# Moving every SBUF tile behind the constants by about 1.6 KB, onto multiples of 4 KB and 64 bytes

## The chip, the cores and the metric

The kernel runs on one core of one Trainium2 chip. The metric is the device time of one execution in microseconds (us), the median of several runs. A core has a matmul engine (PE, TensorE), whose weight loads are listed apart as PEld, a vector engine (DVE), a scalar engine (ACT), GpSimd (POOL) and a queue engine (SP) that issues all transfers here. The engines work on SBUF, a memory of 128 partitions; a tile has the same byte addresses in each partition, and "address" below means the byte offset inside a partition.

## What is computed

Two layers of a decoder trunk over 256 tokens of width 1024, in float32. Each layer is a SwiGLU feed-forward block, a token mixer (sliding-window attention beside an RWKV-7 state recurrence, joined by gates), and a second SwiGLU block, each followed by a residual layer norm:

```python
for l in range(DEPTH):
    x = layer_norm(ALPHA * x + 0.5 * swiglu(x, ffn_w_gu[l, 0], ffn_w_down[l, 0]), ln_g[l, 0], ln_b[l, 0])
    mix, v_first = token_mix(x, w_in[l], b_in[l], ...)
    x = layer_norm(ALPHA * x + mix, ln_g[l, 1], ln_b[l, 1])
    x = layer_norm(ALPHA * x + 0.5 * swiglu(x, ffn_w_gu[l, 1], ffn_w_down[l, 1]), ln_g[l, 2], ln_b[l, 2])
```

with `swiglu(x) = (silu(gate) * up) @ w_down`, `gate, up = split(x @ w_gu)`, 2816 hidden columns.

## The kernel before

**Products in three parts.** Each large product is made of three single-pass matmuls in the format fp32r: weights and activations are split into a high and a low part, and `mm3` adds high x high, high x low and low x high into one PSUM tile. `chunk` brings weights in pieces of 128 x 1024 floats: one transfer (or two) into a buffer `raw`, a cast on ACT into the high part, a subtraction on DVE into the low part. The parts go into the tiles `wh` and `wl` of the pool `wp`, three buffers each; in the feed-forward blocks (and the output projection) `deep=True` makes the chunks go round seven places, of which three are `wh`/`wl`, three lie in tiles of the pool `tp` that only the mixer uses otherwise, and one in the pair `rwh`, `rwl` of the pool `pp`. In the profile the tiles of the last four are all named `ws`. In the mixer all chunks are `wh`/`wl`.

```python
SPARE = (None, ("tp", "wG"), None, ("tp", "wuv", "wbkt"), None, ("tp", "war", "wbk"), ("pp", "rwh", "rwl"))

    def mm3(self, out, a, b, start, stop):
        mm = self.nc.tensor.matmul
        mm(out, a[0], b[0], start=start, stop=False)
        mm(out, a[0], b[1], start=False, stop=False)
        mm(out, a[1], b[0], start=False, stop=stop)
```

These three are lines 140, 141 and 142 of the profile. The second argument is the stationary operand (PEld reads 128 x 128 of it, 512 bytes of each partition), the third the moving one, which PE streams column by column, 4 bytes of each partition for a column.

**Two shapes.** Where the result is wanted with channels on the partitions (the body of the first feed-forward product, PSUM tile `accm`; the mixer's projections, `accm`; its two branch products, `accb`), the weights are stationary and the moving operand is 256 columns, 1024 bytes, of the activations: `xTh` and `xTl` for `accm`, `oTh`, `oTl`, `rwh`, `rwl` for `accb`. Where tokens are on the partitions (the first 512 hidden columns, the down projection, the output projection, PSUM tiles `acc` and `accg`), the activations (`mr`, `cum`, `gt0` and so on) are stationary and the moving operand is 512 columns, 2048 bytes, of a weight chunk. By the loops of the code there are 7104 of these fp32r matmuls: 4992 into `accm` (1536 of them in the mixers), 384 into `accb`, and 1728 with 512 columns. The small matmuls of attention and recurrence are plain fp32.

**Order.** Each engine works through its instructions in program order; in the mixer a table of numbers interleaves the recurrence with pieces of the projections. All transfers are issued from SP.

**Where tiles lie.** Four SBUF pools stand one behind another: `const` (identity, masks), `wp` (`raw`, `wh`, `wl`), `pp` (activations, parameters), `tp` (temporaries). A pool gives each tag as many buffers as it asks for, in the order of first use, and rounds each buffer up to 32 bytes. In front of `wp` stand the constants, among them `nhalf`, one float (4 bytes, 32 as rounded), so that what follows begins 32 bytes past a multiple of 64.

Of the kernel before, what the change touches and what calls it, by code (L numbers as in the profile page):

```python
# [9 lines left out]
F32 = mybir.dt.float32  # L10
# [5 lines left out]
P = 128  # L16
# [11 lines left out]
H = 8  # L28
# [3 lines left out]
NEG = -1e30  # L32
DECAY = math.exp(-0.5)
SPARE = (None, ("tp", "wG"), None, ("tp", "wuv", "wbkt"), None, ("tp", "war", "wbk"), ("pp", "rwh", "rwl"))
HT_TAGS = ("mr", "mk", "ma", "mep", "men", "mg", "cum", "mv", "gt0", "gt1", "gt2", "oTh")


# [12 lines left out]
VEC, VCOLS = {}, 0  # L50
# [6 lines left out]
class Trunk:  # L57
    def __init__(self, tc, ctx, ap):
        self.tc, self.nc, self.ap = tc, tc.nc, ap
        PS = bass.MemoryType.PSUM  # L60
        pool = lambda name, bufs, **kw: ctx.enter_context(tc.tile_pool(name=name, bufs=bufs, **kw))
        self.const = pool("const", 1)
        self.wp = pool("wp", 3)
        self.pp = pool("pp", 1)
        self.tp = pool("tp", 2)
        self.acc = pool("acc", 4, space=PS)
        self.sm = pool("sm", 3, space=PS)
        self.yp = pool("yp", 1, space=PS)
        self.dram = pool("dram", 1, space=bass.MemoryType.DRAM)
        self.n = self.nspare = 0  # L70
        self.first = []
        nc = self.nc
        self.ident = self.const.tile([P, P], F32, tag="ident", name="ident")
        nc.sync.dma_start(self.ident, ap["ident"])
        self.nhalf = self.const.tile([P, 1], F32, tag="nhalf", name="nhalf")
        nc.gpsimd.memset(self.nhalf, -0.5)

    def nm(self, s):
# [3 lines left out]
    def chunk(self, src, shape=(1, D), swap=False, deep=False, fine=1):  # L82
# [4 lines left out]
        if deep:  # L87
            spare = SPARE[self.nspare % len(SPARE)]
            self.nspare += 1
# [153 lines left out]
    def ffn(self, l, f, last, between=None):  # L243


        nc = self.nc
        hT = [[self.m4(HT_TAGS[6 * i + j], F32R) for j in range(6)] for i in range(2)]
        ps = [[None] * NT for g in range(2)]
# [63 lines left out]

    def load_vecs(self, l):

        vec = self.pp.tile([P, VCOLS], F32, tag="vec", name=self.nm("vec"))
        self.nc.sync.dma_start(vec, self.ap["vecs"][l])
        self.nc.gpsimd.tensor_scalar(vec[:, :NHALF], vec[:, :NHALF], 0.5, None, ALU.mult)
        return lambda name, i: vec[:, VEC[name] + i:VEC[name] + i + 1]

    def load_lora(self, l):  # L320
        nc, ap = self.nc, self.ap
        wa = self.pp.tile([P, 512], F32, tag="wa", name=self.nm("wa"))
        nc.sync.dma_start(wa[:64, :], ap["rw_w2"][l])
        nc.sync.dma_start(wa[64:, :], ap["rw_a2"][l])
        g2 = self.pp.tile([P, 512], F32, tag="g2", name=self.nm("g2"))
        nc.sync.dma_start(g2, ap["rw_g2"][l])
        v12 = None
        if l:
            v1 = self.pp.tile([P, 4, 32], F32, tag="v1", name=self.nm("v1"))
            nc.sync.dma_start(v1, ap["rw_v1"][l - 1].rearrange("(k p) r -> p k r", p=P))  # L330
            v2 = self.pp.tile([32, 512], F32, tag="v2", name=self.nm("v2"))
            nc.sync.dma_start(v2, ap["rw_v2"][l - 1])
            v12 = v1, v2
        sk = self.pp.tile([P, H], F32, tag="sink", name=self.nm("sink"))
        nc.sync.dma_start(sk, ap["attn_sinks"][l:l + 1, :].to_broadcast([P, H]))
        return wa, g2, v12, sk

# [694 lines left out]
```

## Time and profile before

| what | value |
|---|---|
| median of 3 runs | 1234.98 us (1234.7 to 1238.6) |
| the profiled execution's own time | 1237.51 us |
| its span, first to last instruction | 1235.6 us |
| PE busy, share of the span | 97% |
| PEld, DVE, ACT, POOL | 87%, 64%, 45%, 6% |
| mean granted TensorE clock | 0.996 of full speed |
| bytes moved, mean rate | 207.81 MB, 168 GB/s |

The span is what the profile divides into stages; the device time lies 1.91 us above it in that execution. "Busy" of an engine is the time in which at least one of its instructions was under way; since matmuls overlap each other, the distance from one matmul's start to the next tells more than the duration of one.

### The profile page before, as it was taken

The page shows a single profiled execution, that of the slowest core. Times are in us where ns is not written, and L with a number is a line of the kernel's source. Part 1 is how long each engine was busy: PE and PEld are TensorE (multiplying, and loading weights), DVE is VectorE, ACT ScalarE, POOL GpSimd, SP SyncE. Part 2 cuts the span into 40 slices and gives each one's busy share as a digit, 9 for nine tenths or more (in the row PEclk, how much of TensorE's full clock was granted, in tenths as well). Part 3 has the DMA queues.
Part 4 walks back from the last instruction along what each step waited for, and adds up shares of the span by engine and source line. Part 5 has one row for each costly group of instructions (what it writes and reads, how often), then busy time and mean ns, then how long its engine had stood idle before and what let it go on. Part 6 is the DMA issues. An engine that isn't in the chain of part 4 may idle for free.

```text
span 1235.6 us, 25429 instructions
## 1 busy us (share of the span) xinstructions
PE 1199.3 (97%) x10756; PEld 1075.5 (87%) x10756; DVE 792.4 (64%) x1174; ACT 550.9 (45%) x771; POOL 71.2 (6%) x96
## 2 busy tenths in 40 slices
PE   7999999999999999999999999999999999999997
PEld 5999888998789689998789998788987896999985
DVE  4555548967857866554666544588678588665544
ACT  5455434544434455443245444254354354554430
POOL 0000000211100000000000000012011000000000
PEclk9999999999999999999999999999999999999999
DMA  8777664442425577666377666364424255776661
GB/s 265 230 242 219 188 188 136 137 122 82 145 76 148 169 229 225 196 185 193 110 230 221 195 197 188 103 187 120 122 72 136 71 159 170 235 222 191 194 194 35
DMA packets 158001, 207.81 MB, mean 168 GB/s; under 512 B 8480, under 2 KB 133024, under 8 KB 157888
## 3 DMA queue, kind: packets, MB, share of 16 engines
q1 hardware_dynamic: 157888, 206.20, 55.1%
q8 instruction: 84, 1.38, 0.5%
q14 instruction: 29, 0.24, 0.1%
HBM read 205.12 MB, written 1.05 MB: 167 GB/s over the span
## 4 chain that ended last, share of the span: by engine, by line
PE 84%; DVE 7%; DMA 4%; issue 2%; ACT 2%; POOL 1%; SPq 0%; POOLq 0%; DVEq 0%; ACTq 0%
PE accm L140 15%; PE accm L142 15%; PE accm L141 15%; PE acc L140 9%; PE acc L141 9%; PE acc L142 8%; DMA raw<-in_w_out_dram 2%; DMA raw<-in_ffn_w_gu_dram 2%; DVE wl L119 1%; PE ps L133 1%; PE ps L724 1%; PE ps L715 1%; PE tr L151 1%; DVE ws L119 1%; PE y L133 1%
## 5 line engine op out<-in xcount | busy, mean ns | idle before, releaser
L119 DVE TENSOR_TENSOR wl<-raw,wh 128x1024 fp32r<-128x1024 f32 (+1 forms) x206 | 241.4, 1176 | 160.8 <-ACT wh L116 158.9
L116 ACT CAST wh<-raw 128x1024 fp32r<-128x1024 f32 x196 | 205.8, 1050 | 269.1 <-PE accm L141 121.0
L119 DVE TENSOR_TENSOR ws<-raw,ws 128x1024 fp32r<-128x1024 f32 (+1 forms) x178 | 201.9, 1139 | 172.2 <-ACT ws L116 170.6
L142 PE MATMUL accm<-xTh,wl 128*128 128x256 f32 x1000 | 286.2, 286 | 3.9 <-issue 2.3
L140 PE MATMUL accm<-xTh,wh 128*128 128x256 f32 x1000 | 289.9, 290 | 0.0
L141 PE MATMUL accm<-xTl,wh 128*128 128x256 f32 x1000 | 285.4, 285 | 0.0
L116 ACT CAST ws<-raw 128x1024 fp32r<-128x1024 f32 x164 | 171.8, 1049 | 204.8 <-DMA raw<-in_ffn_w_gu_dram 68.5
L140 PEld LDWEIGHTS accm<-xTh,wh 128*128 128x128 f32 x1000 | 191.4, 191 | 8.0 <-issue 6.0
L142 PEld LDWEIGHTS accm<-xTh,wl 128*128 128x128 f32 x1000 | 191.8, 192 | 5.1 <-DVE wl L119 2.0
L141 PEld LDWEIGHTS accm<-xTl,wh 128*128 128x128 f32 x1000 | 191.6, 192 | 2.0 <-issue 1.3
L140 PE MATMUL accm<-xTh,ws 128*128 128x256 f32 x664 | 184.0, 277 | 0.0
L142 PE MATMUL accm<-xTh,ws 128*128 128x256 f32 x664 | 183.7, 277 | 0.0
L141 PE MATMUL accm<-xTl,ws 128*128 128x256 f32 x664 | 183.6, 276 | 0.0
L140 PEld LDWEIGHTS accm<-xTh,ws 128*128 128x128 f32 x664 | 125.3, 189 | 0.1
L141 PEld LDWEIGHTS accm<-xTl,ws 128*128 128x128 f32 x664 | 124.6, 188 | 0.1
L142 PEld LDWEIGHTS accm<-xTh,ws 128*128 128x128 f32 x664 | 124.6, 188 | 0.0
L199 POOL TENSOR_SCALAR lnrs<-lnmv 128x1 f32<-128x1 f32 x12 | 5.6, 468 | 780.9 <-DVE lnmv L197 780.9
L142 PE MATMUL acc<-ws,gt 128*128 128x512 f32 x108 | 42.6, 394 | 0.0
L153 ACT CAST xTh<-tr 128x256 fp32r<-128x256 f32 x40 | 13.9, 372 | 55.5 <-PE tr L151 55.1
L142 PE MATMUL acc<-wh,gt 128*128 128x512 f32 x84 | 33.4, 398 | 0.0
L194 DVE SCALAR_TENSOR_TENSOR pre<-acc,x 128x512 f32<-128x512 f32 x24 | 16.5, 688 | 25.2 <-PE acc L142 25.1
L140 PE MATMUL acc<-wh,xTh 128*128 128x512 f32 x56 | 23.0, 413 | 8.0 <-ACT wh L116 7.6
(318 smaller groups left out, 2008.6 us busy)
## 6 DMA issues: line engine op xcount, KB each, us to landing
raw<-in_ffn_w_gu_dram SPq DMA_DIRECT2D x176, 512.0 KB, 4.6
raw<-in_ffn_w_down_dram SPq DMA_DIRECT2D x88, 512.0 KB, 4.3
raw<-in_w_in_dram SPq DMA_DIRECT2D x56, 512.0 KB, 4.4
raw<-in_w_in_dram SPq DMA_DIRECT2D x32, 256.0 KB, 3.1
raw<-in_w_out_dram SPq DMA_DIRECT2D x16, 512.0 KB, 4.4
raw<-in_w_branch_attn_dram SPq DMA_DIRECT2D x16, 256.0 KB, 4.0
raw<-in_w_branch_rwkv_dram SPq DMA_DIRECT2D x8, 512.0 KB, 4.1
lng<-in_ln_g_dram SPq DMA_DIRECT2D x6, 512.0 KB, 3.7
```

The lines of the kernel that those rows point to most:

```text
L116: nc.scalar.copy(wh, raw)
L119: nc.vector.tensor_sub(wl[:, c], raw[:, c], wh[:, c].bitcast(F32))
L133: ins = self.nc.tensor.matmul(*args, **kw)
L140: mm(out, a[0], b[0], start=start, stop=False)
L141: mm(out, a[0], b[1], start=False, stop=False)
L142: mm(out, a[1], b[0], start=False, stop=stop)
L151: nc.tensor.transpose(ps[:, i, :], x_sb[:, (k + i) * P:(k + i + 1) * P], self.ident)
L153: nc.scalar.copy(xh[o], ps[:, :m, :])
L194: nc.vector.scalar_tensor_tensor(pre[:, c], psums[h], scale / ALPHA, self.x[t][:, c], ALU.mult, ALU.add)
L199: nc.gpsimd.tensor_scalar(rs, mv[:, 1:2], LN_EPS / ALPHA ** 2, None, ALU.add)
L715: mm(ps[rb, m, :], ql[lv][rb, m, :], x[rb, m, :], start=True, stop=True)
L724: mm(ps[rb, m, :], bt[rb, m, :], z[rb, m, :], start=True, stop=True)
```

## The change

Three tiles are made larger, and only their first part is used: `nhalf` from 1 to 400 floats, `vec` from 82 to 96 floats, `sink` from 8 to 16 floats.

```diff
+NCONST = 400
-        self.nhalf = self.const.tile([P, 1], F32, tag="nhalf", name="nhalf")
+        self.nhalf = self.const.tile([P, NCONST], F32, tag="nhalf", name="nhalf")[:, :1]
-        vec = self.pp.tile([P, VCOLS], F32, tag="vec", name=self.nm("vec"))
+        vec = self.pp.tile([P, 96], F32, tag="vec", name=self.nm("vec"))[:, :VCOLS]
-        sk = self.pp.tile([P, H], F32, tag="sink", name=self.nm("sink"))
+        sk = self.pp.tile([P, 2 * H], F32, tag="sink", name=self.nm("sink"))[:, :H]
```

No instruction is added, removed or moved: on each of the five engines the built program has the same instructions with the same operands, sizes and waits in the same order. What differs is addresses. Everything behind `nhalf` moves up by 1568 bytes, what lies behind `vec` by 1600, and what lies behind `sink` by 1632. The places of the tiles that the fp32r matmuls read, as the allocator gives them:

| tiles | address before | past a multiple of 64 / of 512 | address after | past a multiple of 64 / of 512 |
|---|---|---|---|---|
| `raw`, `wh`, `wl`, three each | 23008 to 55776 in steps of 4096 | 32 / 480 | 24576 to 57344 | 0 / 0 |
| `xTh`, `xTl` | 59872, 68064 | 32 / 480 | 61440, 69632 | 0 / 0 |
| `oTl`, `mr`, `mk`, `ma`, `mep`, `men` | 80352, 92640 to 109024 | 32 / 480 | 81920, 94208 to 110592 | 0 / 0 |
| `mg`, `cum`, `mv`, `gt0`, `gt1`, `gt2`, `oTh` | 113184 to 137760 | 32 / 32 | 114752 to 139328 | 0 / 64 |
| `rwh`, `rwl` (also `ws`) | 141856, 145952 | 32 / 32 | 143424, 147520 | 0 / 64 |
| `wG`, `wuv`, `wbkt`, `war`, `wbk` (also `ws`) | 165280 to 189856 | 32 / 416 | 166912 to 191488 | 0 / 0 |

Some tiles began at multiples of 64 before already, among them `ident`, at 16512, and the mixer's `wa` and `g2`, at 150400 and 152448.

## Rows read from the trace of the kernel before

**Rows 1.** The page: engines, and the chain that ended last.

```profile
PE 1199.3 (97%) x10756; PEld 1075.5 (87%) x10756; DVE 792.4 (64%) x1174; ACT 550.9 (45%) x771; POOL 71.2 (6%) x96
...
PE 84%; DVE 7%; DMA 4%; issue 2%; ACT 2%; POOL 1%; SPq 0%; POOLq 0%; DVEq 0%; ACTq 0%
```

**Rows 2.** Stretches: us, busy (x instructions) by engine, granted clock, DMA share, GB/s.

```profile
110.00:180.00 70.00, 70.00 (x408) 61.36 (x408) 34.08 (x32) 30.08 (x31) 0.00 (x0) 1.00 0.66 195
240.00:405.00 165.00, 158.15 (x2485) 142.09 (x2484) 119.82 (x232) 70.85 (x129) 18.26 (x21) 0.99 0.42 122
500.00:580.00 80.00, 80.00 (x572) 74.79 (x571) 41.08 (x39) 36.06 (x39) 0.00 (x0) 1.00 0.63 192
```

**Rows 3.** PE, timeline, `wh`/`wl` stationary: start, us of one, instruction.

```profile
62.11 0.28 PE L141 MATMUL accm<-xTl,wh 128*128 128x256 f32 x1
62.23 0.28 PE L142 MATMUL accm<-xTh,wl 128*128 128x256 f32 x1
...
62.95 0.28 PE L142 MATMUL accm<-xTh,wl 128*128 128x256 f32 x1
```

**Rows 4.** The same, `ws` in the tiles of the pool `tp`.

```profile
63.19 0.28 PE L141 MATMUL accm<-xTl,ws 128*128 128x256 f32 x1
63.30 0.28 PE L142 MATMUL accm<-xTh,ws 128*128 128x256 f32 x1
...
64.21 0.28 PE L141 MATMUL accm<-xTl,ws 128*128 128x256 f32 x1
```

**Rows 5.** The same, `ws` in `rwh`, `rwl`, in two passes over them.

```profile
67.12 0.28 PE L142 MATMUL accm<-xTh,ws 128*128 128x256 f32 x1
...
68.48 0.28 PE L142 MATMUL accm<-xTh,ws 128*128 128x256 f32 x1
...
70.03 0.28 PE L140 MATMUL accm<-xTh,ws 128*128 128x256 f32 x1
...
71.33 0.28 PE L142 MATMUL accm<-xTh,ws 128*128 128x256 f32 x1
```

**Rows 6.** The same, 512 moving columns: from `wh`/`wl`, and from `tp`.

```profile
140.00 0.39 PE L141 MATMUL acc<-wl,mr 128*128 128x512 f32 x1
...
142.09 0.39 PE L141 MATMUL acc<-wl,mr 128*128 128x512 f32 x1
...
142.78 0.39 PE L141 MATMUL acc<-ws,mr 128*128 128x512 f32 x1
...
144.86 0.39 PE L141 MATMUL acc<-ws,mr 128*128 128x512 f32 x1
```

**Rows 7.** Plain fp32 on PE: timeline of two windows, and durations min/median/max in ns.

```profile
219.34 0.92 PE L133 MATMUL psl<-xg,g 128*128 128x256 f32 x3
219.34 1.99 PE L133 MATMUL psl<-xg,g 128*128 128x256 f32 x8
...
205.67 0.60 PE L537 MATMUL tr<-ident,gt 128*128 128x128 f32 x4
L537 PE MATMUL tr<-ident,gt x16: 271/273/329, 205.7 to 819.2; 128*128 128x128 f32 x16
```

**Rows 8.** Groups of the page, and `accm` in the two mixers (PE, PEld, DVE, ACT).

```profile
L142 PE MATMUL accm<-xTh,wl 128*128 128x256 f32 x1000 | 286.2, 286 | 3.9 <-issue 2.3
L140 PE MATMUL accm<-xTh,ws 128*128 128x256 f32 x664 | 184.0, 277 | 0.0
...
184.00:425.00 241.00, 106.74 (x768) 96.29 (x768) 1.91 (x4) 13.14 (x28) 0.99 0.42 124
794.00:1042.00 248.00, 107.91 (x768) 96.75 (x768) 1.91 (x4) 13.16 (x28) 0.99 0.41 122
```

**Rows 9.** The page: transfers by tile, number, KB each, us to landing.

```profile
raw<-in_w_in_dram SPq DMA_DIRECT2D x32, 256.0 KB, 3.1
g<-in_rw_g_dram SPq DMA_DIRECT2D x2, 256.0 KB, 3.2
```

## Prediction

> **What bounds the kernel now.** I read the page first: PE is busy for 97% of the span, and 84% of the chain that ended last is PE's [rows 1]. Then the stretches, since that average covers several stages. In the feed-forward blocks PE has no idle time at all (70.00 of 70.00 us, 80.00 of 80.00), while DVE and ACT are busy for half of it or less and transfers for about two thirds; in the mixer PE still works 158.15 of 165 us [rows 2]. So a nanosecond per matmul counts some thousand times, and a gain on any other engine counts only where a stage begins. The granted clock is 1.00 in the feed-forward blocks, the level of 2.4 GHz: a column then lasts 0.417 ns, 256 columns 106.7 ns, 512 columns 213.3 ns.
>
> The timeline of PE shows that it does not reach this. With `wh` and `wl` stationary, seven steps from 62.11 to 62.95 take 0.84 us: 120.0 ns for a matmul of 256 columns [rows 3]. With the `tp` tiles stationary, nine steps from 63.19 to 64.21 take 1.02 us: 113.3 ns [rows 4]. Shape, moving operand and engine are the same; what differs is where the weights lie. With `rwh` and `rwl` it is 113.3 ns in one pass (1.36 us for twelve steps) and 118.2 in another (1.30 us for eleven) [rows 5]. With 512 columns moving it is 232 ns from `wh`/`wl` and 231 from `tp` (2.09 and 2.08 us for nine steps) [rows 6]. Plain fp32, which takes two passes of the clock per column, behaves otherwise: 128 columns in (600 - 273) / 3 = 109 ns, 256 columns in (1.99 - 0.92) / 5 = 0.214 us [rows 7], hence 256 or 512 clock steps and about 2.5 ns. The moving operand there is `ident`, at a multiple of 64, or `xg`, 32 past one, and neither shows more than that.
>
> **How I read these numbers.** 113.3 and 120.0 are 106.7 plus once and twice 6.67 ns, and 6.67 ns is 16 columns, or 64 bytes of a partition. I take SBUF to hand PE 64 bytes of a partition at a time, with just enough speed for one fp32r column per clock. Then 1024 bytes that begin 32 past a multiple of 64 touch 17 such lines, and 17 x 6.67 is 113.3; plain fp32 asks for half that rate, so an extra line is hidden there. The second 6.67 ns comes where the weights that PEld reads for the next matmul meet the moving operand. In the table of addresses, `wh`, `wl`, `xTh` and `xTl` all lie 480 past a multiple of 512 (their inner steps are 512 and 1024 bytes): both streams begin on the same line of the 512, and one gives way once. `tp` lies 64 bytes lower (416), `rwh` 64 higher (32), and the collision is absent or now and then there. This is inference: before, every fp32r operand is 32 past a multiple of 64, so no row shows an aligned one.
>
> **The change part by part.** The larger tiles cost no work: the same instructions, and the unused parts are neither loaded nor set. Transfers and the other engines see new addresses too. 256 KB into `g2`, at a multiple of 64 before, land after 3.2 us and 256 KB into `raw`, 32 past one, after 3.1 [rows 9]; packets differ in length, but nothing there speaks for alignment, and a fraction of 3 us at each of about a dozen stage starts would be a few us at most, so I enter nothing. DVE and ACT are covered by PE, being busy for half the time [rows 2].
>
> For PE, two edits in opposite directions:
>
> *The line.* All fp32r operands begin at multiples of 64, so a matmul of 256 columns needs 16 lines, not 17, and one of 512 needs 32, not 33. That is 6.67 ns for each, down to a floor of 109 (or 214 to 216) ns by rows 7. Bounds from rows: nothing, if the 6.67 ns has another cause; the whole distance to the floor, if alignment ends the collisions too.
>
> *The collision.* `wh` against `xTh` stays at distance 0, `rwh` at 64. The `tp` tiles go from 64 below `xTh` to distance 0 (3072 and 0 past a multiple of 4096, both 0 past one of 512). By rows 3 and 4 that costs these matmuls 6.67 ns. Bounds: 0, and 6.67.
>
> Counts: 3 x 1000 matmuls with `wh`/`wl`, of which 2 x 768 in the mixers, and 3 x 664 with `ws` [rows 8], three quarters of them in `tp` (1494) and one quarter in `rwh`/`rwl` (498); by the code 384 into `accb` and 1728 with 512 columns. So:
>
> 1. `wh`/`wl`, feed-forward: 1464 x 6.67 = 9.8 us saved (120.0 to 113.3).
> 2. `wh`/`wl` and `accb` in the mixers: 1920 x 6.67 = 12.8 us. There the recurrence's chain passes DVE and ACT, and these matmuls fill its gaps; PE is idle for 4% [rows 2]. Some of the gain turns into longer waits; between 0 and 12.8 I take half, 6.4 us.
> 3. `ws` in `tp`: one line less, one collision more: 0.
> 4. `ws` in `rwh`/`rwl`: 113.3 to the floor of 109, 498 x 4.3 = 2.1 us.
> 5. 512 columns: 1728 x 6.67 = 11.5 us, between 0 and two lines, 23.0 (231 is nearer to 34 or 35 lines than to 33, so these collide anyway).
>
> Sum: 29.8 us. The profiled execution took 1237.51 us with a span of 1235.6; the median of the runs, 1234.98, is 2.5 below it, and I count from the median: **1205 us**. With terms 2 and 5 at their ends it is 1187 to 1223.
>
> **The rivals.**
>
> *Only the distance counts, and the 17th step is no matter of alignment* (a cost at each matmul's end that is rounded up to whole lines would look the same). Then the line term is 0, and the `tp` tiles, moved into step with `xTh`, go from 113.3 to 120.0 ns: 1494 x 6.67 = 10.0 us, all in feed-forward blocks where PE is never idle, so **1245 us**. It decides as soon as fewer than about 1500 of the other matmuls gain a line. For it: rows 3 and 4, which show the distance at work and nothing on alignment. Against it: 113.3 is 17 lines without remainder.
>
> *Addresses matter only in the large, or not at all.* `wh` and `xTh` lie within 40 KB of each other, `tp` 100 KB away; if near tiles collide, a move by 1.6 KB changes nothing: **1235 us**, within 0.3% (3.7 us, about what a measurement of this kernel can tell from no change). Against it: `rwh`, 80 KB from `xTh`, shows both 113.3 and 118.2 [rows 5]. [...]
>
> *Alignment ends collisions as well.* Then all go to the floor: 3000 x 11, 1494 x 4.3, 498 x 6 and 384 x 9 ns are 33, 6.4, 3.0 and 3.5 us, 1728 x 16 ns are 27.6: 73 us, less half of the mixers' 20: 63 us, **1172 us**. For it: plain fp32 reaches this floor. [...] Against it: two streams on one line must still take turns.
>
> **How the numbers follow.** The forecast gets 0.48, the floor 0.20, the distance alone 0.20, no effect 0.12. Faster by over 0.3%: 0.68; within it: 0.12; slower: 0.20. To leave out no more than 2 in 10 the range must reach both outer cases: 1172 to 1246, the likeliest case's own being 1187 to 1223.
>
> **What would show each step.** PE's timeline in a feed-forward body: 113.3 ns with `wh`, 113.3 with `tp`, 109 with `rwh`/`rwl`, about 225 with 512 columns, and plain fp32 as before. Right on the line but wrong on the collision: `tp` at 109. The first rival: 120 with both `wh` and `tp`, 231 with 512. The floor: 109 and 216 throughout. If PE idles longer in the feed-forward blocks, with more waits for `raw`, transfers could not follow the faster PE: 512 KB for twelve matmuls at 225 ns are 194 GB/s, against 195 GB/s in rows 2 with a third of the transfer time free, so I don't expect it. The prediction fails most easily if the 6.67 ns is no line.

## The result: 0.7% slower, and the profile after

The changed kernel took 1244.54 us (median of 4 runs, 1243.76 to 1246.68) against 1235.56 for the kernel before beside it (4 runs): a ratio of 1.0072, with an interval of 1.0047 to 1.0097. (Ratios here are those on record and differ slightly from the quotients of the medians; an interval is the 95% one.) The forecast was 1205 us; the rival in which only the distance between tiles counts gave 1245.

The page of the changed kernel (line numbers are two higher than before): the engines, and two groups of matmuls with 256 columns (busy us, mean ns of one, idle before); 512 of the 1000 in the first group belong to the mixers.

```profile
PE 1207.9 (97%) x10756; PEld 1086.5 (87%) x10756; DVE 792.8 (64%) x1174; ACT 552.1 (44%) x771; POOL 72.5 (6%) x96
...
L142 PE MATMUL accm<-xTh,wh 128*128 128x256 f32 x1000 | 290.2, 290 | 0.0
...
L142 PE MATMUL accm<-xTh,ws 128*128 128x256 f32 x664 | 188.0, 283 | 0.0
```

PE has grown by 8.6 us over [rows 1] and its weight loads, PEld, by 11.0; the other engines by 1.3 us at most. Of PE's groups on the page, the one with `ws` as weights has grown, to 283 ns for one from 277 [rows 8]. The one with `wh` has not; before it was:

```profile
L140 PE MATMUL accm<-xTh,wh 128*128 128x256 f32 x1000 | 289.9, 290 | 0.0
```

The timeline of PE after the change shows the steps.

```profile
61.88 0.28 PE L142 MATMUL accm<-xTh,wh 128*128 128x256 f32 x1
...
62.48 0.28 PE L144 MATMUL accm<-xTh,wl 128*128 128x256 f32 x1
62.60 0.28 PE L142 MATMUL accm<-xTh,ws 128*128 128x256 f32 x1
...
63.92 0.28 PE L144 MATMUL accm<-xTh,ws 128*128 128x256 f32 x1
...
70.13 0.28 PE L142 MATMUL accm<-xTh,ws 128*128 128x256 f32 x1
...
71.19 0.28 PE L142 MATMUL accm<-xTh,wh 128*128 128x256 f32 x1
```

With `wh` it is 0.60 us for five steps, 120 ns, as in [rows 3]: no line was saved. With a `tp` tile (62.60 to 63.92) it is 1.32 us for eleven steps, 120 ns, where [rows 4] had 113.3. With `rwh`/`rwl` (70.13 to 71.19) it is 117.8 ns for nine steps, the slower of the two states in [rows 5].

Over the whole trace the mean step went like this. Steps of more than 200 ns (300 with 512 columns) are left out, and a step counts for the weights of the matmul that begins at its end. The order of the chunks gives 1488 matmuls with `tp` tiles and 504 with `rwh`/`rwl`, where the prediction took three quarters and one quarter, 1494 and 498.

| weights, columns | number | before, ns | after, ns | change x number, us |
|---|---|---|---|---|
| `tp`, 256 | 1488 | 114.05 | 119.98 | +8.8 |
| `rwh`/`rwl`, 256 | 504 | 114.51 | 117.70 | +1.6 |
| `wh`/`wl` in feed-forward blocks, 256 | 1464 | 119.41 | 119.98 | +0.8 |
| `wh`/`wl` in the mixers, 256 | 1536 | 119.63 | 119.67 | +0.1 |
| all with 512 columns | 1728 | 231.61 | 230.49 | -1.9 |

The sum is +9.4 us; the spans differ by 9.3 (1244.9 and 1235.6), the medians by 9.0.

### The profile page after: what moved, and what is told of

It is laid out like the page before. It is cut to its first block, busy times and chain, and to the rows that moved or that the text cites. A ratio compares the mean times of both kernels' runs of the same rounds, so it can differ in the third digit from the quotient of the medians.

```text
span 1244.9 us, 25429 instructions
## 1 busy us (share of the span) xinstructions
PE 1207.9 (97%) x10756; PEld 1086.5 (87%) x10756; DVE 792.8 (64%) x1174; ACT 552.1 (44%) x771; POOL 72.5 (6%) x96
## 4 chain that ended last, share of the span: by engine, by line
PE 83%; DVE 8%; DMA 3%; issue 2%; ACT 2%; POOL 1%; SPq 0%; POOLq 0%; DVEq 0%; ACTq 0%
PE accm L142 16%; PE accm L144 15%; PE accm L143 15%; PE acc L144 8%; PE acc L143 8%; PE acc L142 8%; DMA raw<-in_w_out_dram 2%; DVE wl L121 1%; PE ps L135 1%; DMA raw<-in_ffn_w_gu_dram 1%; PE ps L726 1%; ACT wh L118 1%; PE tr L153 1%; PE ps L717 1%; DVE lnst L197 1%
## 5 line engine op out<-in xcount | busy, mean ns | idle before, releaser
L142 PE MATMUL accm<-xTh,ws 128*128 128x256 f32 x664 | 188.0, 283 | 0.0
L144 PE MATMUL accm<-xTh,ws 128*128 128x256 f32 x664 | 187.6, 282 | 0.0
L143 PE MATMUL accm<-xTl,ws 128*128 128x256 f32 x664 | 187.6, 282 | 0.0
L142 PEld LDWEIGHTS accm<-xTh,ws 128*128 128x128 f32 x664 | 127.4, 192 | 0.1
L144 PEld LDWEIGHTS accm<-xTh,ws 128*128 128x128 f32 x664 | 126.8, 191 | 0.0
```

## The experiments

Theory D: what a step costs hangs on the distance, within a period of some hundred bytes, between the tile that PEld reads and the one that PE streams. In the diffs, `gap` is a tile that nothing reads or writes; it is made before all others of its pool, and moves every later tile.

**Alignment alone, from the kernel before.**

```diff
+        self.wp.tile([P, 8], F32, tag="gap", name="gap_wp", bufs=1)
```

> All tiles from the pool wp on move up by 32 bytes, so that every fp32r operand begins at a multiple of 64 as in the changed kernel, but all distances between them stay as they were before (wh to xTh 0, tp to xTh 64 lower). Theory D (only the distance between the stationary and the moving tile counts): 120.0 ns per matmul of 256 columns with wh, 113.3 with the tp tiles, 1235 us as before (within 4). Rival A (begins at multiples of 64 are themselves what slows the changed kernel): tp at 120, about 1244 us. The forecast's line theory, if something in the changed kernel merely hid its gain: wh at 113.3, tp at 109, about 1200 us.

Measured: 1234.99 us against 1234.90, ratio 1.001 (0.9995 to 1.0025). Timeline of PE, 256 columns, all operands at multiples of 64:

```profile
61.75 0.28 PE L142 MATMUL accm<-xTl,wh 128*128 128x256 f32 x1
...
62.35 0.28 PE L141 MATMUL accm<-xTh,ws 128*128 128x256 f32 x1
...
62.58 0.28 PE L143 MATMUL accm<-xTh,ws 128*128 128x256 f32 x1
...
63.60 0.28 PE L143 MATMUL accm<-xTh,ws 128*128 128x256 f32 x1
```

Five steps of 120 ns with `wh` and nine of 113.3 with a `tp` tile, as before. The line term of the prediction is gone, and so is rival A.

**Distance alone, from the kernel before.**

```diff
+        self.tp.tile([P, 16], F32, tag="gap", name="gap_tp", bufs=1)
```

> Only the pool tp moves, by 64 bytes; all fp32r operands stay 32 past a multiple of 64, and tp comes to distance 0 from xTh. Theory D: tp at 120.0 ns, wh at 120.0, rwh/rwl at 113 to 118 as the phase at their start has it, about 1244 us (1494 x 6.67 = 10 us over before). Rival A: nothing is aligned, so tp stays at 113.3 and the time at 1235 us.

Measured: 1244.32 us, ratio 1.0083 (1.0064 to 1.0102). 64 bytes in front of one pool do what the whole change does:

```profile
63.09 0.28 PE L141 MATMUL accm<-xTh,ws 128*128 128x256 f32 x1
...
64.41 0.28 PE L143 MATMUL accm<-xTh,ws 128*128 128x256 f32 x1
```

Eleven steps of 120 ns with a `tp` tile that lies at distance 0 and is not aligned.

**The distance taken back, in the changed kernel.**

```diff
+        self.tp.tile([P, 112], F32, tag="gap", name="gap_tp", bufs=1)
```

> The changed kernel with the pool tp moved by another 448 bytes, so that its tiles lie 64 below xTh again as before the change; every fp32r operand keeps a multiple of 64. Theory D: tp back to 113.3 ns and wh at 120, 1235 us, the same as before within 0.3%. If anything but the distance of tp slowed the changed kernel, part of its 9 us stays.

Measured: 1234.58 us against 1234.74, ratio 0.9992 (0.9979 to 1.0005); `tp` at a mean of 114.06 ns, `wh`/`wl` at 119.6. Nothing of the 9 us stays.

**The other tiles moved apart, from the kernel before.**

```diff
+        self.pp.tile([P, 16], F32, tag="gap", name="gap_pp", bufs=1)
```

> All of the pools pp and tp move by 64 bytes against wp: wh and wl come to lie 64 below xTh and xTl, where the tp tiles lay and stay. Theory D: 113.3 ns with wh as with tp; 1464 matmuls in feed-forward blocks x 6.67 = 9.8 us saved, 1536 in the mixers x 6.67 = 10.2 us of which half counts, rwh/rwl now entered from a free phase and at 113.3 (about 1 us): about 1219 us (1214 to 1225). Rival R (matmuls collide with tiles that lie near, whatever the distance modulo 512): wh stays at 120 ns and the time at 1235 us.

Measured: 1226.73 us, ratio 0.9939 (0.992 to 0.9957): faster, but 8 us where 16 were expected. Rival R falls: in the feed-forward blocks `wh`/`wl` went from 119.4 to a mean of 114.0 ns. In the mixers they went only to 117.2. The timeline of a feed-forward block shows what lies behind it:

```profile
452.22 0.28 PE L141 MATMUL accm<-xTh,ws 128*128 128x256 f32 x1
...
453.28 0.28 PE L141 MATMUL accm<-xTh,ws 128*128 128x256 f32 x1
...
457.02 0.28 PE L142 MATMUL accm<-xTl,ws 128*128 128x256 f32 x1
...
457.61 0.28 PE L141 MATMUL accm<-xTh,ws 128*128 128x256 f32 x1
...
458.29 0.28 PE L141 MATMUL accm<-xTh,wh 128*128 128x256 f32 x1
...
459.65 0.28 PE L141 MATMUL accm<-xTh,ws 128*128 128x256 f32 x1
...
489.57 0.28 PE L141 MATMUL accm<-xTh,wh 128*128 128x256 f32 x1
...
490.93 0.28 PE L141 MATMUL accm<-xTh,ws 128*128 128x256 f32 x1
491.04 0.28 PE L142 MATMUL accm<-xTl,ws 128*128 128x256 f32 x1
...
492.29 0.28 PE L141 MATMUL accm<-xTh,wh 128*128 128x256 f32 x1
```

At one distance, 64 below, nine steps take 1.06 us (117.8 ns) soon after a stage has begun, and twelve take 1.36 (113.3) later, with `wh` as with `tp`. So there are two states. At 457.02 and 457.61 PE is in a pass over `rwh`/`rwl`, which lie 64 above `xTh`, and the state changes within it: five steps of 118 ns up to 457.61, then six of 113.3 up to 458.29, and 113.3 with `wh` and all that follows. By the trace's starts it is so in all four feed-forward blocks: each begins at 117.8 ns or returns to it after the small fp32 matmuls `tr`, changes for the last time in such a pass or at its start, and stays at 113.3 to its end. The mixers have no such chunk, their runs are short, and each begins after small fp32 matmuls; about one in five or fewer of their steps were below 115.5 ns, against four in five or more in the feed-forward blocks.

**Three sweeps of the distance.** `wh` and `wl` are made 32 or 64 bytes wider, so that their three buffers lie at three distances, and gaps set where these begin (the first sweep's edit without its gap in `tp`; the others differ in widths and gaps):

```diff
-            wh = self.wp.tile([P, 1024], F32R, tag="wh", name=self.nm("wh"), bufs=3)
-            wl = self.wp.tile([P, 1024], F32R, tag="wl", name=self.nm("wl"), bufs=3)
+            wh = self.wp.tile([P, 1032], F32R, tag="wh", name=self.nm("wh"), bufs=3)[:, :1024]
+            if not self.n_gap:
+                self.n_gap = self.wp.tile([P, 104], F32, tag="gap2", name="gap2", bufs=1)
+            wl = self.wp.tile([P, 1032], F32R, tag="wl", name=self.nm("wl"), bufs=3)[:, :1024]
```

> The three buffers of wh, and those of wl, lie 96, 64 and 32 bytes below xTh and xTl (modulo 512), and the tp tiles 32 below. If SBUF hands out 64 bytes at a time and collisions are between such pieces, 32 below touches the same piece at half of the time and costs 3 to 7 ns, 64 and 96 below cost nothing (113.3 ns). If the pieces are 32 bytes or less, 32 below costs nothing either and all show 113.3 ns. Time about 1219 us if nothing at 32, 1235 or more if 32 collides like 0.

> The three buffers of wh, and those of wl, begin 256 above, 192 below and 128 below xTh and xTl (modulo 512), the tp tiles 128 below. Theory D with a period of 512 bytes: only distance 0 collides, so 113.3 to 118 ns at all three, and about 1225 us. Theory D with a period of 128 (two lines of 64 taking turns): 128 and 256 are like 0, 120 ns; only 192 is free; about 1245 us.

> The same with 64, 128 and 192 above, and the tp tiles 64 above. Period 512: 113.3 to 118 ns everywhere, about 1225 us. Period 128: 64 and 192 at 113.3 to 118, 128 at 120 ns, and about 1232 us. If the sign counts (64 above showed 113.3 or 118 by its entry, 64 below mostly 113.3), tp at 118 and 1230 us or more.

Measured, one execution each and so without an interval: 1235.47 us (against a median of 1234.9), 1238.12 and 1227.06 (against one execution at 1234.7). Mean steps of 256 columns, worked out from the starts as above, feed-forward blocks and mixers together (bytes by which the weights lie above `xTh`/`xTl`; the column for 0 is from the runs before):

```
 distance   -256   -192   -128    -96    -64    -32      0    +64   +128   +192
 wh, wl    119.5  115.2  118.5  119.9  116.2  116.9  119.6  114.6  118.4  114.9
 tp                      118.5         114.1  116.9  120.0  113.7
```

Neither expected period is right. 0 and 256 are the same, 128 is nearly as dear, and odd multiples of 64 are cheap on either side; 32 is between, and 96, which was to cost nothing, is as dear as 0.

**The disputed steps by themselves.** 62 blocks of 24 matmuls ahead of the kernel's own work; the weights begin `d` above the moving operand, which begins `m` bytes into a tile that lies 32 past a multiple of 64, and has `n` columns. The inner loop:

```diff
+            for _ in range(24):
+                self.nc.tensor.matmul(ps[:, :n], st[:, a:a + P], mv[:, b:b + n], start=True, stop=True)
```

> Ahead of the kernel's own work stand 62 blocks of 24 fp32r matmuls on two weight tiles, whose results nobody reads; the kernel's own result is as before, its time longer by about 180 us. In a block all steps are alike: the weights begin d bytes above the moving operand (modulo 512), which begins m bytes into its tile and has n columns. Theory D: 120 ns at d = 0 and 113 to 118 at d = 64 and 448, with 256 columns; between 0 and 64 a slope or a jump tells how wide the piece is that collides. The 17th step: if it is a fixed cost at each matmul, (n + 16) / 2.4 ns for every n of 128 or more; if it is one step in 17, n / 2.4 x 17 / 16 ns, 56.7 at 128 and 226.7 at 512; if it is a line more because the operand begins 32 past a multiple of 64, it vanishes at m = 32 (109 ns), which the aligned kernel already speaks against.

Timeline of two blocks, `d` = 64 and `d` = 256 (`n` = 256; runs of equal matmuls are one row, with the time from the first start to the last end):

```profile
21.13 2.10 PE L171 MATMUL probe<-wh,wh 128*128 128x256 f32 x17
...
43.73 2.08 PE L171 MATMUL probe<-wh,wh 128*128 128x256 f32 x16
```

(2.10 - 0.28) / 16 is 114 ns, (2.08 - 0.28) / 15 is 120. Means of the last 16 steps of each block, from the trace's starts; the distances stood twice, in rising and in falling order:

```
 d, n=256     0     32     64     96    128    160    192    224    256    320    384    448
 rising           118.4  113.4  117.4  120.2  119.9  113.4  116.7  120.0  117.8  118.6  117.8
 falling  120.3   118.4  117.8  118.5  118.7  120.0  117.8  116.7  120.0  113.3  118.8  117.8

 n          192    240    272    320    384    448    512
 d=64            112.1  123.4  146.7  173.4  202.1  233.4
 d=448    111.7  111.6  126.7  146.7  173.3  200.1  228.7
```

(Two blocks are left empty: the first, whose early steps took 213 ns, and one at a granted clock of 0.56. Left out are those of 64 and 128 columns, and distances of 16, 48, 80, 112 and 480, at 118 to 120 ns.) Odd multiples of 64 take 113.3 or 117.8 ns at one and the same distance; 0 and 256 take 120. At `d` = 64, operands that begin at `m` = 32, a multiple of 64, or at 16 or 48 settle at 113.3 ns, as one 32 past it. Only `m` = 4, which begins both operands 36 bytes past a multiple of 64, takes 120.0, at `d` = 64 and at 448 (where the other three take 117.8 to 118.3). And 113.3 is no line more. A column takes 0.417 ns: (200.1 - 146.7) / 128 between 320 and 448 columns at `d` = 448, at a granted clock of 1.00. What a matmul takes over its columns is neither fixed nor one part in 16, but 6.7 ns at 256 columns, 13.4 at 320 and 384 and 15 to 20 at 512 for these two distances, while 192 and 240 columns, 80 and 100 ns by themselves, take 112. The expectation had none of this, and its 180 us more were 196.

**Fewer weights.** The same with 256 or 512 moving columns and fewer columns of weights, `w`. The inner line:

```diff
+                        self.nc.tensor.matmul(ps[:w, :n], st[:, d // 4:d // 4 + w], mv[:, :n], start=True, stop=True)
```

> Blocks of 24 matmuls ahead of the kernel's own work, their results unread, with 256 or 512 moving columns and 128, 96, 64 or 32 columns of weights, at distances of 64, 0 and 192 bytes. Theory W (the 17th step and the collisions belong to the weight load: it reads 512 bytes of a partition for each matmul, and in the blocks of 192 and 240 columns the step stayed at 111.7 ns, above the 80 and 100 ns of the columns): with 64 or 32 columns of weights the step of 256 columns falls to 107 to 109 ns at every distance, that of 512 to 214 to 216. Theory S (a step is lost at the end of each moving operand, whatever the weights): 113.3 and 226.7 or more remain at 64 and 192 bytes with few columns of weights too.

Timeline of the block with 64 columns of weights at distance 0, and of a piece with 128 there and 512 moving columns:

```profile
49.20 1.98 PE L168 MATMUL probe<-wh,wh 128*64 128x256 f32 x16
...
58.63 0.85 PE L168 MATMUL probe<-wh,wh 128*128 128x512 f32 x3
```

(1.98 - 0.28) / 15 is 113.3 ns, and (0.85 - 0.39) / 2 about 230, as near as hundredths of a us allow. Means of the last 16 steps of each block:

```
 columns of weights      128     96     64     32
 d=64,  256 moving            116.9  119.0  113.4
 d=0,   256 moving     119.9  116.0  113.3  113.3
 d=192, 256 moving     117.8  113.3  113.3  113.3

 d=64,  512 moving     233.3  228.3  232.6  231.7
 d=0,   512 moving     226.7  230.0  229.7  231.7
 d=192, 512 moving     228.9  233.3  228.4  231.2
```

(The first block, whose early steps took 213 ns, is left empty.) At distance 0 the step from 113.3 to 120 goes with the length of the weight load: it is gone with 64 columns of weights or fewer. At distance 64 that is not shown, since the block with 64 columns took 119.0 ns, more than any other there. The step from 106.7 to 113.3 does not go: it is there with 32 columns at all three distances, where theory W expected 107 to 109. So theory W holds for the collision at distance 0 alone and falls for the 17th step; theory S gave the right bounds, and what is behind it stays open. With 512 columns the order is another: 128 columns of weights at distance 0 are the cheapest block.

**Versions that beat both kernels.** All weight tiles 64 above, from the kernel before, and the same from the changed kernel with gaps of 112 and 16 floats:

```diff
+        self.pp.tile([P, 112], F32, tag="gap", name="gap_pp", bufs=1)
+        self.tp.tile([P, 32], F32, tag="gap", name="gap_tp", bufs=1)
```

> From the kernel before, pp moves by 448 bytes and tp by 576, so that all weight tiles lie 64 above xTh and xTl modulo 512, and the stationary activations of the 512-column matmuls 64 below wh, wl and tp. By the steps measured in the sweeps: wh 120 to about 114.7 (1464 in feed-forward blocks x 5.3 = 7.8 us, 1536 in the mixers x 5.3 at half = 4 us), tp as before, rwh/rwl 0.4 us, 512 columns from 231.6 to about 230.2 (2 us), the two branches worse by up to 0.5 us: about 1221 us (1217 to 1226). If the phase in which a run of matmuls begins decides more than the distance, 1227 as with 64 below.

> The changed kernel with pp moved by 448 bytes and tp by 512: the same distances as in the run before, and every operand of the fp32r matmuls at a multiple of 64. Theory D: the same time as that run within 0.3%, about 1221 us, and so 23 us faster than the changed kernel. If alignment matters after all once the collisions are gone, the two differ.

Measured: 1226.22 us, ratio 0.9933 (0.9907 to 0.996), and 1223.43, ratio 0.9914 (0.9885 to 0.9942), both against 1234.57. The intervals overlap: alignment is again without effect that these runs show. All 256-column steps into `accm` have means of 115.4 to 115.5 ns, those of 512 columns 229.3: `wh` gained 4, the 512 columns 2, but `tp` lost 1.4 to the step of 117.8 ns. The mean is one of two states, not a step of its own: by the trace's starts the second half of a feed-forward block is at 117.8 ns in the first and second block and at 113.3 in the third and fourth, and in the aligned version at 117.8 in the second and third. With all weights at one distance PE stays in a state until the next small matmuls `tr`, of which none come in the second half, and the distance does not decide which state it is. A whole block of 864 such matmuls at 117.8 ns takes 3.8 us longer than at 113.3, an estimate from these two steps.

**Distances chosen apart for the two shapes**, with 64 bytes ahead of `pp`, 384 ahead of `mr` and 128 ahead of `mg`:

```diff
+        self.gaps = {"mr": 96, "mg": 32}
...
+        if tag in self.gaps:
+            self.pp.tile([P, self.gaps.pop(tag)], F32, tag="gap_" + tag, name="gap_" + tag, bufs=1)
```

> Distances chosen apart for the two shapes: wh, wl and tp 64 below xTh as in the run with pp moved by 64 (113.9 ns in the feed-forward blocks there), rwh 64 above, and the stationary activations of the 512-column matmuls at 64 below or 128 above the weights (229 to 230 ns in the sweeps, against 232.8 at 64 above). From 1226.7 us of that run, about 1700 x 2.5 ns = 4 us less: 1222 us (1218 to 1227). If the phase of the 512-column matmuls decides more than their distance, 1227.

Measured: 1225.76 us, ratio 0.992 (0.9903 to 0.9936), against 1234.74. In the feed-forward blocks 256 columns take 113.7 to 114.0 ns, as wanted; with `rwh`/`rwl` at the other sign again, all four feed-forward blocks end at 113.3. But 512 columns take 232.3 where 229 to 230 were expected. For them the distance does not settle the step; what does was not found.

## Why the prediction was wrong

**The step that failed is the line term.** The prediction took 113.3 ns for 17 lines of 64 bytes, the author's estimate from 106.7 plus 6.67, which fits without remainder, and entered 6.67 ns saved for nearly every fp32r matmul: 9.8, 6.4 and 11.5 us in its terms 1, 2 and 5, and the line of term 3. The 106.7 is measured: where the trace of the kernel before shows a granted clock of 0.50 (324.2 to 327.6 and 938.6 to 942.0 us), such a matmul takes 213 ns, twice as much, and the probe has 0.417 ns for a column, 2.4 columns in 1 ns. No run shows a line of 64 bytes, or two streams that take turns on one. What alignment alone measured cannot be told from zero: a ratio of 1.001 (0.9995 to 1.0025), by the lower end of the interval at most 0.6 us saved, where terms 1, 2 and 5 had 27.7 of the 29.8; and 113.3 ns with an aligned operand as with one 32 past. The text said that no row showed an aligned fp32r operand and still gave the reading 0.68; a number that fits is weaker than a row that varies the thing in question. Begins of 16 and 48 bytes into a tile cost nothing either (`m` in the probe, 113.3 ns), while 4 bytes cost 6.7 ns at a distance of 64 (120.0).

**The collision was right, in place and size.** `tp` at distance 0 was to cost 6.67 ns; [rows 4] went from 113.3 to 120.0, 8.8 us over the trace against 10.0 worked out. Moving that pool alone makes the loss, moving it back removes it. With the line term at nothing the prediction's own sum is its first rival, 1245 us, to which it gave 0.20. That 1244.54 us lies between 1172 and 1246 is no merit of the forecast: its own case ended at 1223, and the range was stretched to take in that rival. The collision itself was inferred from an agreement of addresses; its period, 512 bytes, was wrong (256 is as dear as 0), which made no difference here.

**Term 4 was wrong in sign.** `rwh`/`rwl` were to gain 2.1 us down to a floor of 109 ns and lost 1.6. It also started from 113.3 ns for all of these, though [rows 5] had 118.2 in one pass of two. The floor came from plain fp32, which takes 0.82 ns for a column, (214 - 109) / 128 by [rows 7], about twice the 0.417 of fp32r; no fp32r matmul of 256 columns in any run had a steady step below 113.3. The loss is a state that lasts: before, the pass that followed a `tp` tile was at 113.3 and the one that followed `wh` at 118.2 [rows 5]; now all that precedes them is at 120, and both are at 117.8.

**What held.** Transfers and the other engines cost nothing that can be seen: apart from PE and its weight loads no engine's busy time grew by more than 1.3 us, and PE's idle time, 37.0 us of the span against 36.3, did not grow with it.

## What to carry to other kernels

Where matmuls run back to back and reload their weights each time, look at the steps between starts, grouped by the addresses of both SBUF operands; here a gap of 64 to 576 bytes was worth 0.6 to 0.9%, and a tidy alignment cost 0.7%. Before rounding tiles up, work out which distances change: a padding that aligns everything can bring two streams into step, as here `tp` with `xTh`, from 113.3 to 120.0 ns. And a change that can act in two ways deserves one run for each, since the sum told nothing about either.

## What the runs showed of the hardware

The step from one fp32r matmul to the next hangs on the distance between the operand that PE streams and the one that PEld loads, by up to 6.7 ns in 113 with 256 columns and 128 columns of weights. In the probe and the sweeps it is 119.5 to 120.3 ns at distances of 0 and 256 bytes, 118.4 to 120.2 at 128, 119.9 to 120.0 at 160 above, 119.9 at 96 below, and 113.3 to 113.4 at 64, 192 and 320, odd multiples of 64, in the better of their two states; at distance 0 with 64 or fewer columns of weights it is 113.3. The blocks of equal matmuls, with no other work on PE between them, show that it is the distance between these two operands: 113.3 against 120.0 ns at equal shapes and a distance of 64 instead of 0. That the streaming and the loading disturb each other is an inference from these steps; how SBUF serves them is not shown.

At odd multiples of 64 there are two steady states, 113.3 and 117.8 ns, and the history decides between them: the same block gave one when the distances rose and the other when they fell. Where all weights lay at one distance, PE kept its state from one interruption by `tr` to the next; where chunks at 64 above came among those at 64 below, every feed-forward block went to 113.3 at one of them and stayed. That is what two traces of each kind show, and no run tests it by itself. Open are the reason for the second state, what sets the 512-column steps (block means from 226.7 to 233.4 ns), and why fp32r with 256 columns never came below 113.3.
